# Two PSUM rings for two jobs: the embedding projections beside the last out-projection norm chain, and three norm chains traced between GEMM steps

## The chip, the cores and the metric

One NeuronCore of one Trainium2 chip. The metric is the device time of one execution in microseconds. The kernel before takes 2876.89 us (median of 3 runs, 2875.72 to 2878.07).

## What is computed

One layer of a hybrid encoder, in float32, on two batches with shared weights: a prompt of 512 tokens (P) and a sample of 1024 tokens (S, two groups g of 512). Cut to what matters here:

```python
mix = concat([y_ssd, y_hy], -1) @ w_out                       # 2048 -> 1024, "out-projection"
h = h + rmsnorm(mix, norm_mix_post)
u = rmsnorm(h, norm_ffn_pre)
ff = (silu(u @ w_gate) * (u @ w_up)) @ w_down                 # 1024 -> 2816 -> 1024
h = h + rmsnorm(ff, norm_ffn_post)
gate = sigmoid(rmsnorm(h, ple_norm_pre) @ w_ple_gate)
e = p_l @ w_ple_proj                                          # 256 -> 1024, "embedding projection"
h = h + rmsnorm(gate * e, ple_norm_post)
```

## The kernel before

Matmuls keep float32 accuracy by splitting each operand into a high and a low part and adding three products (`mm3`, L301 to L303). A weight arrives by DMA from the SP queue as `wst`; ScalarE (ACT) copies it into `whi` (L292) and GpSimd (POOL) subtracts to get `wlo` (L293). A streamed activation arrives as `mx` and is split into `mh` (ACT, L325) and `ml` (VectorE, DVE, L326).

The program is written with a tile framework. A tile belongs to a pool and a tag, and a tag owns a fixed number of buffers, a **ring**: a new tile of the tag waits until the tile that held its buffer has been read for the last time. The framework's scheduler orders each engine's instructions once, when the program is built, from the order of the trace, the dependences, and a priority (`high_priority()`); on the chip each engine then runs its list in that order. PSUM's eight banks are three rings: `g` (2 buffers of 2 banks, `gps()`), `a` of pool m (1 bank) and `a` of pool x (3 banks). `aps()` takes `a` from whichever pool `self.apool` names.

After the mixers, the sample's part runs so:

- `out_group(S, 0)` and `out_group(S, 1)`: the out-projection as a streamed GEMM (`stream_gemm`), two column halves of eight steps each. The second half's four accumulators are three `a` of pool x and one `g`.
- After each group `out_post` calls `post`, a **norm chain**: per tile of 128 tokens (order 0, 2, 1, 3) a sum of squares on ACT (L316, into `junk`), the power -0.5 on POOL (L309), scale by the gain row (L1054), add of the residual tile `t` (L1055), which goes to DRAM (L1056), a second sum of squares, scale (L333), and eight transposes on TensorE (L339, from `acc` into two `a`), from which ACT and DVE make the operands `bh` and `bl` of the next GEMM with `stage` and `wsum` between (L129, L137, L325, L326; class `Sums`). `post` is traced as a whole at high priority.
- `ple_proj(S, 0)` and `(S, 1)`: the embedding projection. Per group two loads of p (L1328, into `mx`), two sets of four transposes (L1332, each into one `a`), their split into `mh` and `ml` (128x256), 48 matmuls of 128x512 into four `g`, and eight copies to `mx` (L1346) that go to DRAM as `e` (L1347, issued from the ACT queue). The tag `mx` is a ring of two, and loads and results share it.
- `gate_up`: gate and up as products of a Strassen-like scheme over summed operands (DVE, L1210), a first job on group 0 alone, then one on group 1 alone, then both groups. Its first product's weight sum (`mx<-wst,wst`, L1210) is again a tile of the ring `mx`.
- `down_group(S, 0)`, `(S, 1)`: the streamed GEMM with w_down, then `post` again, then the embedding gate.

In `build`, `self.apool` is pool x from the second half of `out_group(S, 0)` to the end, so the transposes of the norm chains, those of `ple_proj` and the products of `gate_up` all take `a` from the ring of three, in the order of the trace.

Of the kernel before, what the change touches and what calls it, by code (L numbers as in the profile page):

```python
# [18 lines left out]
D = 1024  # L19
# [147 lines left out]
class Kern:  # L167
# [868 lines left out]
    def post(self, pool, acc, row, res, t0, dst, gain=None, u=None, tags=("t4",) * 4, last=False):  # L1036
# [4 lines left out]
        rts = {}  # L1041
# [85 lines left out]
    def ffn(self, q, g, pool, u):  # L1127
# [21 lines left out]
        self.post(pool, acc2, "norm_ffn_post", q.h1, g * 512, q.h2, "ple_norm_pre", v)  # L1149
        return v  # L1150

    def stream_gemm(self, rows, nk, wsrc, evac):


        for nch in range(2):
# [15 lines left out]
            for t in ORDER:  # L1171
                evac(nch, t, pss[t])
            yield
# [19 lines left out]

    def out_group(self, q, g, pool, acc):
# [3 lines left out]
    def out_post(self, q, g, pool, acc):  # L1198
        u = Sums(self, pool)
        self.post(pool, acc, "norm_mix_post", q.x, g * 512, q.h1, "norm_ffn_pre", u)  # L1200
        return u

    def gate_up(self, q, jobs):
# [98 lines left out]
        for job in jobs:  # L1302
            for p in pair(*job):
# [8 lines left out]
    def down_group(self, q, g, pool, u):  # L1312

        acc = self.new_acc(pool)
        for _ in self.stream_gemm(self.streamed(pool, q.hid, g), NF, self.I["w_down"][0], self.keep(acc)):
            pass
        v = u()
        self.post(pool, acc, "norm_ffn_post", q.h1, g * 512, q.h2, "ple_norm_pre", v)
        return v
# [53 lines left out]
    def build(self):  # L1373
# [43 lines left out]
        with self.pool("mix_s", side="right") as mp, ExitStack() as right:  # L1417
# [3 lines left out]
            with self.pool("tail_u") as tu, self.pool("tail_p") as tp:  # L1421
# [12 lines left out]
                u = self.ffn(P, 0, pl, u)  # L1434
# [3 lines left out]
                next(out)  # L1438
                self.ple_post(P, 0, pl, self.ple(P, 0, pl, u))
            self.apool = self.pools["x"][0]  # L1440
            next(out)
            with self.pool("blocks") as tb:
                pb = pm | tags(tb, ("bh", 14), ("bl", 14))
                po |= pb
                us = [self.out_post(S, 0, po, acc)]
                acc = self.new_acc(po)
                for _ in self.out_group(S, 1, po, acc):
                    pass
                us.append(self.out_post(S, 1, po, acc))
                pe = pm | {"et": pm["mx"], "hh": pm["mh"], "hl": pm["ml"]}  # L1450
                for g in range(2):
                    for _ in self.ple_proj(pe, S, g):
                        pass
                right.close()
                with self.pool("hid_s", side="right") as tr:
                    ph = pb | tags(tr, ("wsum", 3), ("sc", 5), ("gt", 6))
                    pe = pb | {"wsum": pm["mx"], "gt": pm["mh"], "sc": pm["ml"]}
                    both = dict(enumerate(us))
                    self.gate_up(S, [(p, m, {g: both[g] for g in gs}) for p, gs, ms in (
                        (pe, [0], (0,)), (ph, [1], (0,)), (ph, [0, 1], range(2, NF, 2))) for m in ms])  # L1460
# [39 lines left out]
```

## Time and profile before

| | |
|---|---|
| median of 3 runs | 2876.89 us |
| the profiled execution | 2871.61 us, its span 2869.8 us |
| TensorE busy | 2685.3 us, 94% of the span |
| VectorE / ScalarE / GpSimd busy | 61% / 46% / 48% |
| mean granted TensorE clock | 0.978 |
| chain that ended last | PE 70%, DVE 14%, DMA 7%, issue 4%, POOL 3%, ACT 2% |

Times inside the profile are microseconds from the span's start. The page has one line per engine with its busy time, the span in 40 slices with the clock that TensorE was granted (9 is 90% or more of the full 2.4 GHz, 5 is half), and the chain of work that ended last. The last out-projection GEMM ends at about 1958, its norm chain and the two embedding projections take the stretch to about 2030, `gate_up` runs to about 2498 and the down-projection from about 2481.

### The profile page before, as it was taken

To read this page: it belongs to the slowest core of one execution; us is meant where nothing else is said; L and a number is where in the kernel's file an instruction comes from. 1 tells how busy PE (TensorE), PEld (TensorE's weight loads), DVE (VectorE), ACT (ScalarE), POOL (GpSimd) and SP (SyncE) were. 2 spreads that over 40 slices of the span, in tenths; PEclk is the share of its full clock that TensorE was granted. 3 is DMA by queue.
4 is the path that set the end of the run, shared out by engine and by line. 5 is a ranking of instruction groups with operands and counts; after the bars stand their busy time and mean duration, and the time that the engine had idled before them with its cause. 6 is when DMAs were issued, how large, how long until landed. Compare 5 with 4: busy or idle time off the path is not lost.

```text
span 2869.8 us, 41652 instructions
## 1 busy us (share of the span) xinstructions
PE 2685.3 (94%) x14696; PEld 2260.9 (79%) x14696; DVE 1753.3 (61%) x2893; ACT 1328.9 (46%) x2564; POOL 1388.9 (48%) x1137
## 2 busy tenths in 40 slices
PE   7999999999999989799999899886799999899998
PEld 5987888778887767588788777664799999877776
DVE  6767996977667887956766742664443434225345
ACT  4534445763333564645444444554433333345453
POOL 4445554433453555534444444553554444445464
PEclk9999999999999999899999999998999999999999
DMA  5545555744335575778888775564332222366664
GB/s 168 179 139 134 150 182 187 219 143 117 110 106 165 169 256 191 221 204 207 195 210 202 184 226 178 191 225 140 102 90 84 79 78 86 122 200 205 204 205 180
DMA packets 446203, 475.85 MB, mean 166 GB/s; under 512 B 29153, under 2 KB 330025, under 8 KB 443691
## 3 DMA queue, kind: packets, MB, share of 16 engines
q1 hardware_dynamic: 340923, 347.34, 39.7%
q0 software_dynamic: 25920, 63.97, 9.9%
q10 hardware_dynamic: 79152, 61.88, 6.8%
q8 instruction: 116, 1.90, 0.3%
q14 instruction: 92, 0.75, 0.1%
HBM read 346.54 MB, written 91.95 MB: 153 GB/s over the span
## 4 chain that ended last, share of the span: by engine, by line
PE 70%; DVE 14%; DMA 7%; issue 4%; POOL 3%; ACT 2%; SPq 0%; DVEq 0%; ACTq 0%; POOLq 0%
PE g L301 18%; PE g L303 17%; PE g L302 17%; PE a L302 3%; PE a L303 3%; PE a L301 3%; DMA mx<-mix_s 2%; PE a L700 2%; PE a L973 1%; DVE E L615 1%; DVE b L692 1%; POOL wlo L293 1%; PE a L628 1%; PE a L404 1%; DVE W L619 1%
## 5 line engine op out<-in xcount | busy, mean ns | idle before, releaser
L293 POOL TENSOR_TENSOR wlo<-wst,whi 128x512 fp32r<-128x512 f32 (+1 forms) x556 | 801.1, 1448 | 778.2 <-ACT whi L292 698.6
L292 ACT ACTIVATE whi<-wst 128x512 fp32r<-128x512 f32 (+1 forms) x556 | 346.7, 629 | 546.5 <-PE g L302 345.6
L301 PE MATMUL g<-uh,whi 128*128 128x512 f32 (+1 forms) x1232 | 493.8, 401 | 8.1 <-DVE cv L393 3.8
L303 PE MATMUL g<-uh,wlo 128*128 128x512 f32 (+1 forms) x1232 | 492.0, 399 | 0.0
L302 PE MATMUL g<-ul,whi 128*128 128x512 f32 (+1 forms) x1232 | 491.3, 399 | 0.0
L301 PE MATMUL g<-bh,whi 128*128 128x256 f32 x1056 | 293.7, 284 | 18.6 <-DVE gt L1210 7.7
L303 PE MATMUL g<-bh,wlo 128*128 128x256 f32 x1056 | 294.5, 281 | 0.8 <-POOL wlo L293 0.8
L302 PE MATMUL g<-bl,whi 128*128 128x256 f32 x1056 | 295.3, 281 | 0.0
L301 PEld LDWEIGHTS g<-uh,whi 128*128 128x128 f32 x1232 | 233.5, 190 | 67.5 <-issue 10.1
L303 PEld LDWEIGHTS g<-uh,wlo 128*128 128x128 f32 x1232 | 232.9, 189 | 54.0 <-issue 5.8
L302 PEld LDWEIGHTS g<-ul,whi 128*128 128x128 f32 x1232 | 233.0, 189 | 53.3 <-issue 6.9
L326 DVE TENSOR_TENSOR ml<-mx,mh 128x512 fp32r<-128x512 f32 x152 | 126.0, 831 | 222.3 <-ACT mh L325 217.9
L393 DVE SCALAR_TENSOR_TENSOR cv<-g,cols,cv 128x510 f32<-128x510 f32 (+3 forms) x192 | 193.0, 1006 | 64.0 <-ACT cv L387 61.9
L285 POOL DMA_DIRECT2D wlo<-wst x132 | 115.7, 934 | 210.0 <-ACT wlo L284 203.3
L301 PEld LDWEIGHTS g<-bh,whi 128*128 128x128 f32 x1056 | 198.2, 190 | 23.7 <-DVE gt L1210 9.9
L303 PEld LDWEIGHTS g<-bh,wlo 128*128 128x128 f32 x1056 | 200.7, 190 | 1.1 <-POOL wlo L293 1.1
L302 PEld LDWEIGHTS g<-bl,whi 128*128 128x128 f32 x1056 | 200.7, 190 | 0.1
L303 PE MATMUL g<-whi,ul 128*128 128x264 f32 (+1 forms) x576 | 190.3, 331 | 1.3 <-DVE rs_t L308 1.3
L302 PE MATMUL g<-wlo,uh 128*128 128x264 f32 (+1 forms) x576 | 191.3, 332 | 0.0
L309 POOL TENSOR_TENSOR rs_t<-rs_t,nhalf 128x1 f32<-128x1 f32 (+2 forms) x112 | 121.1, 1083 | 143.0 <-DVE rs_t L308 141.7
L301 PE MATMUL g<-whi,uh 128*128 128x264 f32 (+1 forms) x576 | 189.3, 330 | 0.0
L301 PE MATMUL g<-whi,mh 128*128 128x512 f32 x412 | 168.7, 409 | 20.0 <-ACT mh L325 14.7
(328 smaller groups left out, 6021.9 us busy)
## 6 DMA issues: line engine op xcount, KB each, us to landing
wst<-in_w_in SPq DMA_DIRECT2D x192, 256.0 KB
wlo<-wst POOLq DMA_DIRECT2D x132, 256.0 KB, 5.0
wst<-in_w_down SPq DMA_DIRECT2D x132, 256.0 KB
wst<-in_w_out SPq DMA_DIRECT2D x96, 256.0 KB
wst<-in_w_gate SPq DMA_DIRECT2D x92, 256.0 KB
wst<-in_w_up SPq DMA_DIRECT2D x92, 256.0 KB
mx<-hid_s SPq DMA_DIRECT2D x88, 256.0 KB
rw<-rows_s SPq DMA_DIRECT2D x32, 512.0 KB
```

What stands on the lines that cost most here:

```text
L285: nc.gpsimd.dma_start(lo, w, accum_op=ALU.add)
L292: nc.scalar.activation(hi, w, AF.Copy)
L293: (eng or nc.gpsimd).tensor_tensor(out=lo, in0=w, in1=hi.bitcast(F32), op=ALU.subtract)
L301: nc.tensor.matmul(ps, lh, rh, start=first, stop=False, skip_group_check=shared)
L302: nc.tensor.matmul(ps, lh, rl, start=False, stop=False, skip_group_check=shared)
L303: nc.tensor.matmul(ps, ll, rh, start=False, stop=last, skip_group_check=shared)
L309: nc.gpsimd.tensor_tensor(out=t[:, :w], in0=t[:, :w], in1=self.nhalf[:, :w], op=ALU.pow)
L326: self.nc.vector.tensor_tensor(out=lo, in0=ps, in1=hi.bitcast(F32), op=ALU.subtract)
L393: nc.vector.scalar_tensor_tensor(out[:, a:b], ps[:, a + d:b + d], wcol(w), out[:, a:b], ALU.mult, ALU.add)
L404: nc.tensor.transpose(ps[:, j * 128:(j + 1) * 128], srcs[i + j], self.ident)
L615: nc.vector.scalar_tensor_tensor(E[:, h], rw[:, 0, h], dbf[:, c, gh:gh + 1], rw[:, 1, h], ALU.add, ALU.min)
L700: nc.tensor.matmul(ps[:, r, c], fw[:, r0 + r, c], sig[:, r0 + r], start=True, stop=True)
```

## The change

Four edits:

1. `post` becomes a generator, `post_steps`, which yields after the first sums of squares and after each tile. For three chains (the prompt's after its FFN, the sample's group 0 after `out_group(S, 0)`, and the sample's group 0 after `down_group(S, 0)`) the steps are now traced between the steps of the GEMM that follows, by `half`, without the high priority. `stream_gemm` yields after every step for that.
2. The last out-projection chain, and that of `down_group(S, 1)`, are traced as a whole at high priority as before (`rush`).
3. `ple_proj(S, 0)`, `ple_proj(S, 1)` and `gate_up`'s first job take `a` from pool m, the ring of one; later jobs take it from pool x as before.
4. The out-projection's own pool is closed before the embedding projections are traced, not after.

No instruction is added or removed: the five engines' lists hold the same rows in another order.

```diff
     @urgent
-    def post(self, pool, acc, row, res, t0, dst, gain=None, u=None, tags=("t4",) * 4, last=False):
+    def post(self, *args, **kw):
+        for _ in self.post_steps(*args, **kw):
+            pass
+
+    def post_steps(self, pool, acc, row, res, t0, dst, gain=None, u=None, tags=("t4",) * 4, last=False):
...
-        rs = {t: self.rstd(self.sumsq(pool, acc[t]), D) for t in ORDER}
+        for t in ORDER:
+            rs[t] = self.rstd(self.sumsq(pool, acc[t]), D)
+        yield
         for i, t in enumerate(ORDER):
             add(t)
             if i > 0:
                 norm(ORDER[i - 1])
                 if i < 3:
                     load(ORDER[i + 1])
+            yield
         norm(ORDER[3])
+        yield
...
+    def half(self, gemm, chain=iter(())):
+
+        for done in gemm:
+            next(chain, None)
+            if done:
+                return
+        for _ in chain:
+            pass
...
         for job in jobs:
+            self.apool = self.pools["m" if job[0] is early else "x"][0]
             for p in pair(*job):
...
+    def rush(self, chain):
+        with self.tc.high_priority():
+            for _ in chain:
+                pass
...
-                us = [self.out_post(S, 0, po, acc)]
+                u0, chain = self.out_post(S, 0, po, acc)
                 acc = self.new_acc(po)
-                for _ in self.out_group(S, 1, po, acc):
-                    pass
-                us.append(self.out_post(S, 1, po, acc))
-                pe = pm | {"et": pm["mx"], "hh": pm["mh"], "hl": pm["ml"]}
-                for g in range(2):
-                    for _ in self.ple_proj(pe, S, g):
-                        pass
+                out = self.out_group(S, 1, po, acc)
+                self.half(out, chain)
+                self.half(out, chain)
+                u1, chain = self.out_post(S, 1, po, acc)
+                self.rush(chain)
                 right.close()
                 with self.pool("hid_s", side="right") as tr:
                     ph = pb | tags(tr, ("wsum", 3), ("sc", 5), ("gt", 6))
                     pe = pb | {"wsum": pm["mx"], "gt": pm["mh"], "sc": pm["ml"]}
-                    both = dict(enumerate(us))
+                    pe |= {"et": pm["mx"], "hh": pm["mh"], "hl": pm["ml"]}
+                    self.apool = self.pools["m"][0]
+                    for g in range(2):
+                        for _ in self.ple_proj(pe, S, g):
+                            pass
+                    both = {0: u0, 1: u1}
...
-                    vs = [self.down_group(S, g, pe, lambda: Quarters(
-                        *[[self.T(pe, [128, 4, 256], t, F32R) for _ in range(4)] for t in ("bh", "bl")]))
-                        for g in range(2)]
-                    for g in range(2):
-                        self.ple_post(S, g, pe, self.ple(S, g, pe, vs[g]))
+                    v0, chain = self.down_group(S, 0, pe)
+                    v1, chain = self.down_group(S, 1, pe, chain)
+                    self.rush(chain)
+                    for g, v in ((0, v0), (1, v1)):
+                        self.ple_post(S, g, pe, self.ple(S, g, pe, v))
```

What this does to the built order. First TensorE's list right behind the last matmul of the out-projection (`g_3656`). The `a` tiles 3789 to 3810 are the norm chain's transposes, 3816 and 3818 those of the embedding projection's group 0, `g_3825` its first result. Before:

```order
L303 MATMUL g_3656_18190<-whi_3751_18547,ml_3746_18536 128x512
L339 MATMUL a_3789_18644<-ident_1_105,acc_3551_17793 128x128 x4
L339 MATMUL a_3791_18651<-ident_1_105,acc_3551_17793 128x128 x4
L339 MATMUL a_3797_18670<-ident_1_105,acc_3553_17795 128x128 x4
L339 MATMUL a_3799_18681<-ident_1_105,acc_3553_17795 128x128 x4
L339 MATMUL a_3804_18711<-ident_1_105,acc_3552_17794 128x128 x4
L339 MATMUL a_3806_18718<-ident_1_105,acc_3552_17794 128x128 x4
L339 MATMUL a_3808_18726<-ident_1_105,acc_3554_17796 128x128 x4
L339 MATMUL a_3810_18737<-ident_1_105,acc_3554_17796 128x128 x4
L1332 MATMUL a_3816_18761<-ident_1_105,mx_3815_18759 128x128 x4
L1332 MATMUL a_3818_18772<-ident_1_105,mx_3817_18770 128x128 x4
L301 MATMUL g_3825_18793<-whi_3820_18783,mh_3811_18755 128x512
```

and with the change, where L1356 is the old L1332:

```order
L303 MATMUL g_3656_18190<-whi_3751_18547,ml_3746_18536 128x512
L1356 MATMUL a_3816_18765<-ident_1_105,mx_3815_18763 128x128 x4
L301 MATMUL g_3825_18797<-whi_3820_18787,mh_3811_18759 128x512
L302 MATMUL g_3825_18797<-wlo_3821_18788,mh_3811_18759 128x512
L303 MATMUL g_3825_18797<-whi_3820_18787,ml_3813_18761 128x512
L301 MATMUL g_3825_18797<-whi_3823_18793,mh_3812_18760 128x512
L302 MATMUL g_3825_18797<-wlo_3824_18794,mh_3812_18760 128x512
L1356 MATMUL a_3818_18776<-ident_1_105,mx_3817_18774 128x128 x4
...
L339 MATMUL a_3789_18644<-ident_1_105,acc_3507_17631 128x128 x4
L339 MATMUL a_3791_18651<-ident_1_105,acc_3507_17631 128x128 x4
L301 MATMUL g_3837_18847<-whi_3832_18837,mh_3811_18759 128x512
L302 MATMUL g_3837_18847<-wlo_3833_18838,mh_3811_18759 128x512
```

The embedding projection's group 0 now starts ahead of the chain's first transposes, and its 48 matmuls stand between the chain's eight sets; group 1 starts behind the last set, as it did.

On ACT the same place. Before, from the split of the weight `wst_3854` on, the chain has the engine to itself for 21 rows:

```order
L292 ACTIVATE whi_3855_18915<-wst_3854_18913 128x512
L316 ACTIVATE junk_3778_18614,ss_3777_18613<-acc_3552_17794 128x1024
L316 ACTIVATE junk_3781_18620,ss_3780_18619<-acc_3554_17796 128x1024
L316 ACTIVATE junk_3784_18629,ss_3783_18628<-t4_3769_18597 128x1024
L316 ACTIVATE junk_3787_18638,ss_3786_18637<-t4_3770_18599 128x1024
L129 ACTIVATE stage_3790_18649<-a_3789_18644 128x512
L325 ACTIVATE bh_3753_18579<-stage_3790_18649 128x4x128
```

and with the change the splits (`mh`), the copies out (L1370, the old L1346) and their stores (L1371, the old L1347) stand between:

```order
L292 ACTIVATE whi_3855_18919<-wst_3854_18917 128x512
L325 ACTIVATE mh_3811_18759<-a_3816_18765 128x256
L316 ACTIVATE junk_3778_18614,ss_3777_18613<-acc_3508_17632 128x1024
L316 ACTIVATE junk_3781_18620,ss_3780_18619<-acc_3510_17634 128x1024
L325 ACTIVATE mh_3812_18760<-a_3816_18765 128x256
L316 ACTIVATE junk_3784_18629,ss_3783_18628<-t4_3769_18597 128x1024
L316 ACTIVATE junk_3787_18638,ss_3786_18637<-t4_3770_18599 128x1024
L325 ACTIVATE mh_3811_18759<-a_3818_18776 128x256
L1370 ACTIVATE mx_3826_18804<-g_3825_18797 128x512
L1371 DMA e_s_82<-mx_3826_18804 128x512
L325 ACTIVATE mh_3812_18760<-a_3818_18776 128x256
L1370 ACTIVATE mx_3827_18813<-g_3825_18797 128x512
```

DVE's list changes in the same way. The lists of the other two chains that are now traced in steps beside the GEMMs of the prompt's tail and of `out_group(S, 1)` stay as they were but for a few neighbours that change places.

Last, the SP queue at the start of the down-projection: gain rows and residual tiles of the next chain, and the streamed activations. Before:

```order
L321 DMA row_4797_25249<-in_norm_ffn_post 128x1024
L321 DMA row_4798_25251<-in_ple_norm_pre 128x1024
L321 DMA row_5117_26463<-in_norm_ffn_post 128x1024
L1045 DMA t4_4799_25253<-h1_s_80 128x1024
L1045 DMA t4_4800_25255<-h1_s_80 128x1024
L1045 DMA t4_4821_25314<-h1_s_80 128x1024
L1187 DMA mx_4548_24275<-hid_s_83 128x512
L1187 DMA mx_4557_24317<-hid_s_83 128x512
```

and with the change, L1196 and L1050 being the old L1187 and L1045:

```order
L321 DMA row_4815_25303<-in_norm_ffn_post 128x1024
L1196 DMA mx_4548_24275<-hid_s_83 128x512
L321 DMA row_4816_25305<-in_ple_norm_pre 128x1024
L321 DMA row_5117_26463<-in_norm_ffn_post 128x1024
L1196 DMA mx_4557_24317<-hid_s_83 128x512
L277 DMA wst_4599_24473<-in_w_down 128x512
L277 DMA wst_4602_24479<-in_w_down 128x512
L1050 DMA t4_4817_25307<-h1_s_80 128x1024
L277 DMA wst_4611_24521<-in_w_down 128x512
L1050 DMA t4_4818_25309<-h1_s_80 128x1024
L1050 DMA t4_4863_25464<-h1_s_80 128x1024
L1196 DMA mx_4560_24323<-hid_s_83 128x512
```

The first streamed block moves from behind six large loads to behind one, the second from behind six to behind three; the third stays behind all six.

## Rows read from the trace of the kernel before

**Rows 1.** The page: the span, each engine's busy time, and the clock that TensorE was granted in 40 slices.

```profile
span 2869.8 us, 41652 instructions
PE 2685.3 (94%) x14696; PEld 2260.9 (79%) x14696; DVE 1753.3 (61%) x2893; ACT 1328.9 (46%) x2564; POOL 1388.9 (48%) x1137
PEclk9999999999999999899999999998999999999999
```

**Rows 2.** Who TensorE waited for from 1955 to 2045: what waited, for what, us in total, times, longest.

```profile
PE a L339 <- DVE acc L333: 14.6, 2, 13.0
PE a L339 <- DVE rs_t L308: 7.0, 1, 7.0
PE a L1332 <- DMA mx<-in_p_sample: 5.4, 2, 4.3
PE g L301 <- ACT mx L1346: 4.6, 7, 1.2
PE g L301 <- ACT ml L1249: 4.1, 1, 4.1
```

**Rows 3.** Busy time by stretch: stretch, its us, busy us of each engine (with instructions), granted clock, DMA share, GB/s.

```profile
1955.00:1972.00 17.00, 4.04 (x19) 3.14 (x18) 12.19 (x14) 9.65 (x18) 10.95 (x10) 0.68 0.32 108
1972.00:1990.00 18.00, 9.10 (x38) 7.55 (x37) 14.91 (x23) 11.18 (x21) 3.74 (x4) 0.59 0.34 117
1990.00:2010.00 20.00, 13.11 (x49) 8.99 (x48) 5.11 (x11) 8.56 (x16) 3.81 (x3) 0.93 0.44 144
2010.00:2030.00 20.00, 16.71 (x68) 12.39 (x68) 2.06 (x5) 5.87 (x13) 0.00 (x0) 0.86 0.29 105
2090.00:2480.00 390.00, 386.60 (x3272) 383.66 (x3271) 157.64 (x173) 134.77 (x233) 188.86 (x137) 1.00 0.28 83
```

**Rows 4.** The chain that ended last, from 1950 to 2050, in order of time: start, us, what.

```profile
1957.20 0.26 PE g L303
...
1972.22 4.42 DMA t<-in_x_sample
...
1989.50 0.79 PE g L301
...
2003.43 2.54 DMA e_s<-mx
2006.06 0.60 ACT mx L1346
2006.68 2.60 DMA e_s<-mx
2009.34 2.65 DMA mx<-in_p_sample
2012.12 1.09 PE a L1332 x4
2013.21 0.43 PE g L301
...
2030.53 2.00 DMA e_s<-mx
2032.70 0.79 DVE mx L1210
```

**Rows 5.** Instructions in order of time around the start of the chain: start, us, engine, line, operation, shapes, count, idle time before and what ended it.

```profile
1957.74 0.40 PE L303 MATMUL g<-whi,ml 128*128 128x512 f32 x1
1960.36 0.64 ACT L292 ACTIVATE whi<-wst 128x512 fp32r<-128x512 f32 x1
1962.73 2.28 DVE L1054 SCALAR_TENSOR_TENSOR acc<-acc,rs_t,row 128x1024 f32<-128x1024 f32 x1 [0.44 <-POOL rs_t L309]
1965.04 1.23 DVE L1055 TENSOR_TENSOR t<-acc,t 128x1024 f32<-128x1024 f32 x1
1971.10 3.65 PE L339 MATMUL a<-ident,acc 128*128 128x128 f32 x16 [12.96 <-DVE acc L333]
```

**Rows 6.** Groups of instructions from 1955 to 2032, shapes kept apart: count, busy us, mean ns of one, idle time before and what ended it.

```profile
L325 ACT ACTIVATE mh<-a 128x256 fp32r<-128x256 f32 x8 | 3.0, 381 | 7.0 <-PE a L1332 5.3 <-DVE ml L326 1.7
L326 DVE TENSOR_TENSOR ml<-a,mh 128x256 fp32r<-128x256 f32 x8 | 3.3, 420 | 18.2 <-ACT mh L325 18.2
L1346 ACT ACTIVATE mx<-g 128x512 f32<-128x512 f32 x16 | 8.9, 595 | 13.7 <-PE g L303 13.3 <-DMA e_s<-mx 0.4
```

**Rows 7.** The start of `gate_up`, instructions in order of time on ACT and POOL.

```profile
2042.57 0.37 ACT L1249 ACTIVATE ml<-g 128x256 f32<-128x256 f32 x1
...
2035.51 5.88 POOL L293 TENSOR_TENSOR wlo<-wst,whi 128x512 fp32r<-128x512 f32 x4
```

**Rows 8.** The start of the down-projection, instructions in order of time on SP, TensorE and ACT; a stretch of the same place by busy time, as in Rows 3.

```profile
2501.30 0.33 SPq L321 DMA_DIRECT2D row<-in_norm_ffn_post  x1
2504.45 0.93 SPq L1187 DMA_DIRECT2D mx<-hid_s  x2
2505.63 0.40 PE L303 MATMUL g<-whi,ml 128*128 128x512 f32 x1
2513.47 0.80 PE L301 MATMUL g<-whi,mh 128*128 128x512 f32 x1 [7.44 <-ACT mh L325]
2517.82 1.30 ACT L325 ACTIVATE mh<-mx 128x512 fp32r<-128x512 f32 x2 [3.68 <-DMA mx<-hid_s]
...
2508.00:2512.00 4.00, 0.00 (x0) 0.00 (x0) 0.00 (x0) 0.00 (x0) 0.08 (x1) 0.83 1.03 396
```

More of the change, by code (lines that the diff above doesn't have):

```diff
@@ L1148, in ffn @@
         v = self.new_u(pool, 4)
-        self.post(pool, acc2, "norm_ffn_post", q.h1, g * 512, q.h2, "ple_norm_pre", v)
-        return v
+        return v, self.post_steps(pool, acc2, "norm_ffn_post", q.h1, g * 512, q.h2, "ple_norm_pre", v)
     def stream_gemm(self, rows, nk, wsrc, evac):
@@ L1170, in stream_gemm @@
                     self.mm3(pss[t], [r[:, t * 128:(t + 1) * 128] for r in lhs[i]], ws[i], k == 0, k == nk - 1)
-            for t in ORDER:
-                evac(nch, t, pss[t])
-            yield
+                if k0 + 2 == nk:
+                    for t in ORDER:
+                        evac(nch, t, pss[t])
+                yield k0 + 2 == nk
     def keep(self, acc):
@@ L1199, in out_post, with gate_up @@
         u = Sums(self, pool)
-        self.post(pool, acc, "norm_mix_post", q.x, g * 512, q.h1, "norm_ffn_pre", u)
-        return u
-    def gate_up(self, q, jobs):
+        return u, self.post_steps(pool, acc, "norm_mix_post", q.x, g * 512, q.h1, "norm_ffn_pre", u)
+    def gate_up(self, q, jobs, early):
         nc, I = self.nc, self.I
@@ L1310, in gate_up, with down_group @@
             pass
-    def down_group(self, q, g, pool, u):
+    def down_group(self, q, g, pool, chain=iter(())):
         acc = self.new_acc(pool)
-        for _ in self.stream_gemm(self.streamed(pool, q.hid, g), NF, self.I["w_down"][0], self.keep(acc)):
-            pass
-        v = u()
-        self.post(pool, acc, "norm_ffn_post", q.h1, g * 512, q.h2, "ple_norm_pre", v)
-        return v
+        gemm = self.stream_gemm(self.streamed(pool, q.hid, g), NF, self.I["w_down"][0], self.keep(acc))
+        for _ in range(2):
+            self.half(gemm, chain)
+        v = Quarters(*[[self.T(pool, [128, 4, 256], t, F32R) for _ in range(4)] for t in ("bh", "bl")])
+        return v, self.post_steps(pool, acc, "norm_ffn_post", q.h1, g * 512, q.h2, "ple_norm_pre", v)
+    def rush(self, chain):
+        with self.tc.high_priority():
+            for _ in chain:
+                pass
     def ple_proj(self, pool, q, g):
@@ L1433, in build @@
                 self.dma_lo = True
-                u = self.ffn(P, 0, pl, u)
+                u, chain = self.ffn(P, 0, pl, u)
                 self.dma_lo = False
@@ L1437, in build @@
                 out = self.out_group(S, 0, po, acc)
-                next(out)
+                self.half(out, chain)
                 self.ple_post(P, 0, pl, self.ple(P, 0, pl, u))
             self.apool = self.pools["x"][0]
-            next(out)
+            self.half(out)
             with self.pool("blocks") as tb:
@@ L1444, in build @@
                 po |= pb
[L1445 removed]
+                u0, chain = self.out_post(S, 0, po, acc)
                 acc = self.new_acc(po)
[L1447 to L1453 removed]
+                out = self.out_group(S, 1, po, acc)
+                self.half(out, chain)
+                self.half(out, chain)
+                u1, chain = self.out_post(S, 1, po, acc)
+                self.rush(chain)
                 right.close()
```

4 lines of the change are left out of this document (2 added, 2 removed).

## The prediction

> **What bounds the kernel now.** I read the page first: TensorE is busy for 94% of the span, at nearly full clock [rows 1], so time can come only from stretches in which it is idle or slowed. The stretches show where those are. From 2090 to 2480 it is busy for 386.6 of 390.0 us at clock 1.00; from 1955 to 1990 it is busy for 13 of 35 us at 0.68 and 0.59 [rows 3]. The waits of 1955 to 2045 name what it waited for: 21.6 us for the scale step and the power step of the norm chain, 5.4 us for the loads of p, 4.6 us for copies to `mx`, 4.1 us for a copy in `gate_up` [rows 2]. Last, the chain that ended last: the GEMM's last matmul at 1957.2, then norm-chain steps only until 1989.50, where the embedding projections' first matmul starts, and then their matmuls, copies, stores and loads until 2032.5 [rows 4]. So two pieces of work run one behind the other: a norm chain of 32 us that leaves TensorE idle, and two projections of 43 us that don't need the chain. They are in line because all their transposes take `a` from one ring in the order of the trace.
>
> **The change part by part.** No row is added, so the cost is all in what now waits for what. The change is worth what the order makes of three places.
>
> *The last norm chain.* I walk through the new order with the old durations. Group 0's first transposes follow the last matmul, which ends at 1958.1 [rows 5], and take 1.09 us [rows 4]: 1959.3. ACT gives `mh` (0.38) behind the weight split of 1960.36, so at 1961.4; DVE gives `ml` (0.42) behind the scale step that starts at 1962.73 and takes 2.28, so at 1965.4, and the second `ml` one add (1.23) later, at 1967.3 [rows 5, 6]. Pool m has one bank, so the second set of transposes waits for that: 1968.4. A ring of three would not have waited; here it costs little, since TensorE has nothing else. From then on the 48 matmuls, 0.23 us apart, are 11.2 us of work, and the chain's eight sets about 8 (sixteen transposes took 3.65 [rows 5]). Three `ml` on DVE ahead of the chain's first scale by the second gain put the chain's first transposes from 1971.1 to 1971.9. Its second half waits for two residual tiles, whose loads (4.42 us before DVE goes on [rows 4]) start as much later. On ACT eight copies (0.60 each [rows 6]), four `mh` and eight store issues stand among the chain's steps, some 9 us; carried through, the chain's last two scales come 3 to 4 us later than before and its last transposes end at about 1991. That costs nothing by itself: its operands are group 1's, which `gate_up`'s first job doesn't read. The ring `mx` of two decides the rest. A copy needs its buffer's store to have landed, 2.54 to 2.60 us from its issue [rows 4], and the copies wait in ACT's list behind chain steps; I get the last copy of group 0 at about 1992 instead of 2006.06. Group 1's loads then need a store and a load, 2.6 and 2.65 us [rows 4], one behind the other: its two sets of transposes come at about 1995 and 1999 where they came at 2009.9 and 2012.12. Seven matmuls now stand ahead of the second set, and the first six after 2012.12 ran at half clock, 0.43 apart [rows 4], which costs 1.2 us that a busier TensorE may keep. From there the list is the old one. I take **14 us**. Bounds: nothing, if filler and chain only take turns; 28 us, if the 43 us of projections began at 1961 with nothing of the chain in their way.
>
> All that follows hangs on the projections' end: the first weight sum of `gate_up` waits for `mx` until 2032.7 [rows 4], and the weights' buffers come free by its own steps, so it moves along.
>
> Here a rule speaks against the change. What the rows show: each copy followed its matmuls, and only 0.4 us of ACT's idle time before the sixteen copies was for a store [rows 6]. The Trainium skill, Perfetto Trace Analysis, section Per-engine timelines, says that ScalarE, VectorE and GpSimd take their instructions strictly in order and TensorE nearly so. By that rule a copy that waits for a store now holds the norm chain behind it; in my walk it does so three times in group 0, and the rule taken to its end is the slow rival below. The Trainium skill, DMA: Bandwidth & Descriptors, section Anatomy of one DMA, gives a transfer a fixed cost of about 2.0 us; that would make each of these three waits 0.6 us shorter than the rows do and the gain an estimated 16 us. The rows decide.
>
> *The start of `gate_up`.* TensorE stood 4.1 us for a copy that ended at 2042.94 behind a weight split on ACT [rows 2, 7]. In the new list that copy stands one place earlier, where its input is ready, 3 us sooner. But POOL's splits run back to back there, four in 5.88 us [rows 7], in an unchanged order, and TensorE, at 1.4 us for a product of twelve, would soon wait for them. Between 0 and 3 us I take **1**, near POOL's row. Against it stands pool m's single bank for the two products that take an `a`; the second needs the first read by DVE, which came long before its weight was split, so 0.
>
> *The start of the down-projection.* TensorE stops at 2506.0 and waits 7.44 us for the first `mx`, issued at 2504.45 behind six loads of 512 KB [rows 8]; the engines move 396 GB/s there. Now it stands behind one load: 0.75 MB from 2501.3, so landed by about 2505.5 and split by 2507. The second block, behind three, comes at about 2510.4. The third stays behind everything, 4.6 MB at that rate, and comes at about 2517.5, as before (2517.82 [rows 8]). So TensorE does two blocks earlier and waits 4 us ahead of the third. Before, the third started at about 2520.9: 2513.47, 24 matmuls of 0.23, and 1.8 us for half clock. The gain is 3.4 us, or 1.7 if the new wait brings the half clock too (7.4 us of idling did [rows 8]). I take **2**.
>
> *The three chains traced in steps.* Two of them keep their order but for neighbours that change places, and the GEMMs beside them cover those: 0, with 1 us either way. The third is the one whose loads moved above. Closing the pool earlier frees space that only `gate_up`'s second job takes, 20 us later: 0.
>
> Sum: 17 us. The profiled execution took 2871.6 by its own time (span 2869.8), so 2854.6; the median of the runs is 5.3 above that execution. **Predicted: 2860 us.**
>
> **The rivals.** *Less overlap* (0.13). TensorE, thinly loaded from 1959 to 1975, stays at half clock through group 0, as it was at 0.68 and 0.59 [rows 3]. The 48 matmuls then take 0.43 instead of 0.23, 9.6 us more, of which about half lies in waits; with nothing gained at the down-projection the gain is 8: 2869. For it: the clock of those rows. Against it: the waits for DVE and the loads are there anyway.
>
> *More overlap* (0.08). The copies on ACT slip in without waits and group 0 keeps its own pace: 25 us, 2852. Against it: the second residual loads, which nothing hastens.
>
> *Slower: the chain and the filler hold each other* (0.05). Place: ACT between 1961 and 1995. If each of group 0's copies waits its 2.6 us for a store with the chain's step behind it, and TensorE's next filler matmul waits for a `g` that this copy frees, the 32 us and group 0's 17 run in line as before, and the single bank adds its wait twice: 8 us from 1959.3 to 1967.3, 3 to 4 in group 1. The forecast turns at the point where group 0's last copy comes after 2006; with both waits unhidden that gives some 8 us more, 2885. Against it: only three of eight copies meet a store in the walk.
>
> *Nothing moves* (0.04): TensorE's list has changed, but if the filler is late (p not loaded, weights not split) the chain comes first all the same, and what the down-projection gains at its start is lost to DMA at the third block: 2876. Against it: p's loads were issued before 1955.
>
> **How the numbers follow.** About 0.2%, 5.8 us, is what a measurement of this kernel can tell from no change. The forecast (a gain of 10 to 23 us) has 0.70. More overlap is all faster; of less overlap (2 to 10 us) about two thirds are. Faster: 0.70 + 0.08 + 0.09 = 0.87. Same: 0.04 + 0.04 = 0.08. Slower: 0.05. The range takes in most of less overlap and of more, 2851 to 2871.
>
> **What would show it.** Right: TensorE's wait of 13.0 us for the scale step falls to the few us around the chain's first transposes; embedding matmuls stand between the chain's transposes; the second loads of p are issued at about 1992 to 1996 and the first sum of `gate_up` comes near 2018; idle time at the down-projection's start breaks in two. Wrong: the chain's last transposes after 2000, ACT idle for stores with chain steps behind them, or a new wait at `gate_up`'s start that takes back what came before.

## The result and the profile after

The changed kernel takes 2862.46 us (median of 5 runs, 2855.3 to 2865.8), the kernel before 2876.89 (5 runs beside it). The ratio is 0.9944, with a 95% interval of 0.9928 to 0.9960: 11.5 to 20.7 us faster. The forecast was 2860, with a range of 2851 to 2871.

The profiled execution took 2855.3 us, 16.3 less than that of before. It is the lowest of the five, so places are compared inside it and not against the median. The page, as in [rows 1]:

```profile
span 2853.5 us, 41647 instructions
PE 2691.4 (94%) x14696; PEld 2264.9 (79%) x14696; DVE 1751.1 (61%) x2893; ACT 1328.7 (47%) x2564; POOL 1389.5 (49%) x1137
PEclk9999999999999999989999999998899999999999
```

The shares hardly move; the gain has to be looked for by place. Four marks cut both traces: A, the out-projection's last copy (ACT `acc<-g`); B, `gate_up`'s first weight sum (DVE `mx<-wst,wst`); C, its last product (DVE `gt<-g,gt`); D, the 91st split of a streamed activation (DVE `ml<-mx,mh`). In order of time, the first three of before:

```profile
1959.88 0.60 ACT L1177 ACTIVATE acc<-g 128x512 f32<-128x512 f32 x1
...
2029.64 0.69 DVE L1210 TENSOR_TENSOR mx<-wst,wst 128x512 f32<-128x512 f32 x1 [14.68 <-DMA e_s<-mx]
...
2491.38 0.69 DVE L1210 TENSOR_TENSOR gt<-g,gt 128x512 f32<-128x512 f32 x1 [2.90 <-PE g L303]
```

and all four of the change:

```profile
1958.61 0.60 ACT L1186 ACTIVATE acc<-g 128x512 f32<-128x512 f32 x1
...
2013.27 0.69 DVE L1227 TENSOR_TENSOR mx<-wst,wst 128x512 f32<-128x512 f32 x1 [12.90 <-DMA e_s<-mx]
...
2476.53 0.69 DVE L1227 TENSOR_TENSOR gt<-g,gt 128x512 f32<-128x512 f32 x1 [2.94 <-PE g L303]
...
2552.22 0.69 DVE L326 TENSOR_TENSOR ml<-mx,mh 128x512 fp32r<-128x512 f32 x1 [0.50 <-ACT mh L325]
```

D of before is at 2568.91. The differences of the marks:

| stretch | before | change | moved | forecast |
|---|---|---|---|---|
| start to A | 1959.9 | 1958.6 | -1.3 | 0 |
| A to B, last chain and projections | 69.8 | 54.7 | -15.1 | -14 |
| B to C, `gate_up` | 461.7 | 463.3 | +1.5 | -1 |
| C to D, start of the down-projection | 77.5 | 75.7 | -1.8 | -2 |
| D to the end | 300.9 | 301.3 | +0.4 | 0 |

The stretches that answer to [rows 3], each placed 1.4 us earlier (columns as there):

```profile
1953.60:1970.60 17.00, 11.34 (x38) 7.69 (x37) 12.34 (x17) 11.56 (x23) 10.23 (x10) 0.70 0.37 123
1970.60:1988.60 18.00, 12.10 (x56) 9.14 (x55) 12.44 (x18) 12.04 (x23) 5.68 (x6) 0.91 0.60 206
1988.60:2008.60 20.00, 15.68 (x59) 10.73 (x58) 9.75 (x17) 9.80 (x19) 1.26 (x1) 0.83 0.36 126
...
2073.00:2463.00 390.00, 386.90 (x3269) 383.97 (x3267) 159.81 (x175) 135.97 (x235) 188.78 (x137) 1.00 0.27 82
```

In the first two TensorE is now busy for 23 of 35 us instead of 13, and in the second its clock is 0.91 instead of 0.59. TensorE's waits from 1955 to 2030 answer to [rows 2] (what waited, for what, us in total, times, longest):

```profile
PE g L301 <- ACT mx L1370: 5.9, 5, 3.2
PE g L301 <- DVE mh L1227: 3.8, 1, 3.8
PE g L301 <- ACT mh L325: 3.2, 2, 2.8
PE g L303 <- DVE rs_t L308: 2.9, 1, 2.9
PE a L1356 <- DMA mx<-in_p_sample: 2.8, 1, 2.8
...
PE a L339 <- DVE acc L333: 1.4, 1, 1.4
```

The 21.6 us for the chain's scale and power steps are 1.4 plus a wait of 2.9 that has the power step's name but ends with an `ml` behind a scale on DVE. The wait for a copy is longer than it was. TensorE's list, in order of time, against the times of [rows 4, 5]:

```profile
1956.69 0.60 PE L1356 MATMUL a<-ident,mx 128*128 128x128 f32 x4
...
1965.76 1.09 PE L1356 MATMUL a<-ident,mx 128*128 128x128 f32 x4
...
1971.22 1.03 PE L339 MATMUL a<-ident,acc 128*128 128x128 f32 x8
...
1989.48 1.04 PE L339 MATMUL a<-ident,acc 128*128 128x128 f32 x8
...
1993.27 0.66 PE L1356 MATMUL a<-ident,mx 128*128 128x128 f32 x4 [2.75 <-DMA mx<-in_p_sample]
...
1997.48 1.09 PE L1356 MATMUL a<-ident,mx 128*128 128x128 f32 x4 [0.36 <-DVE ml L326]
```

The chain's last transposes before, for comparison:

```profile
1985.38 2.32 PE L339 MATMUL a<-ident,acc 128*128 128x128 f32 x8 [1.65 <-DVE acc L333]
```

The chain's transposes begin where they did, at 1971, and its last ones end at 1990.5 instead of 1987.7; between them group 0 of the projections is done. Group 1's two sets come at 1993 and 1997 instead of 2010 and 2012.

### The profile page after: what moved, and what is told of

It is laid out like the page before. It is cut to its first block, busy times and chain, and to the rows that moved or that the text cites. A ratio compares the mean times of both kernels' runs of the same rounds, so it can differ in the third digit from the quotient of the medians.

```text
span 2853.5 us, 41647 instructions
## 1 busy us (share of the span) xinstructions
PE 2691.4 (94%) x14696; PEld 2264.9 (79%) x14696; DVE 1751.1 (61%) x2893; ACT 1328.7 (47%) x2564; POOL 1389.5 (49%) x1137
## 4 chain that ended last, share of the span: by engine, by line
PE 71%; DVE 14%; DMA 6%; issue 4%; POOL 2%; ACT 2%; SPq 1%; DVEq 0%; POOLq 0%; ACTq 0%
PE g L301 18%; PE g L303 17%; PE g L302 17%; PE a L301 3%; PE a L302 3%; PE a L303 3%; PE a L700 2%; DVE E L615 1%; PE a L973 1%; DVE b L692 1%; PE a L628 1%; PE a L404 1%; DVE W L619 1%; DVE ml L326 1%; POOL wlo L293 1%
```

## The experiments

All stand beside runs of the kernel before on the same chip. They ran on three chips, so from one experiment to another the ratios count more than the medians; places come from one profiled execution of each kernel. The first four take the change apart.

**The ring alone.** The kernel before with one edit:

```diff
+                self.apool = self.pools["m"][0]
                 for g in range(2):
                     for _ in self.ple_proj(pe, S, g):
                         pass
+                self.apool = self.pools["x"][0]
```

> The kernel before with one edit: the two embedding projections take `a` from pool m; `gate_up` takes all its products from pool x, and no chain is traced in steps. Theory (the ring alone joins the chain and the projections): from the last copy of the out-projection to `gate_up`'s first weight sum 55 us, as with the whole change (54.7), not 69.8 as before; from the last `gt` product of `gate_up` to the 91st `ml` of the streamed activations 77.5 us as before, since the down-projection keeps its old load order; time 2863 to 2866. Rival (the steps and the earlier closed pool are needed too): the first stretch stays above 62 us and the time within 3 us of the kernel before.

Measured: 2864.09 us, ratio 0.9951 (0.9935 to 0.9967); A to B 54.1, C to D 77.4. The ring alone makes the overlap, and all of it.

**The steps alone.** The change without its ring of one:

```diff
-                    self.apool = self.pools["m"][0]
                     for g in range(2):
...
-            self.apool = self.pools["m" if job[0] is early else "x"][0]
+            self.apool = self.pools["x"][0]
```

> The whole change, but the embedding projections and `gate_up`'s first job take `a` from pool x as before. Theory: the first stretch is 69 to 70 us again, the stretch around the start of the down-projection 75.7 instead of 77.5, and the time 1 to 3 us below the kernel before, which the runs can hardly tell from no change. Rival (the steps themselves let the projections in): the first stretch falls below 65 us.

Measured: 2875.15, ratio 0.9993 (0.9980 to 1.0006); A to B 70.2, C to D 75.8. Its waits from 1955 to 2030 are those of [rows 2]:

```profile
PE a L339 <- DVE acc L333: 14.6, 2, 13.0
PE a L339 <- DVE rs_t L308: 6.8, 1, 6.8
PE a L1356 <- DMA mx<-in_p_sample: 5.8, 2, 4.6
```

So the steps move the start of the down-projection, by 1.7 us, and nothing else that shows, and the two parts add up. The chain's priority has no part in it: built without `rush` for this chain, or with the projection of group 0 traced ahead of the chain, all five engines' lists are row for row those of the change (built, not run).

**`gate_up`'s first job on the ring of three:**

```diff
-            self.apool = self.pools["m" if job[0] is early else "x"][0]
+            self.apool = self.pools["x"][0]
```

> The whole change, but `gate_up`'s first job takes `a` from pool x; the lists of all engines stay word for word those of the change. Theory 1 (the 1.5 us that `gate_up` took longer come from copies and the table load on ACT and from TensorE's clock, not from the ring of one): from the first weight sum to `gate_up`'s last product 463 us as with the change, time within 2 us of the change. Theory 2 (the single bank makes a product wait): that stretch falls to 461 or 462 us and the idle time of 3.8 us ahead of a product in the first job goes.

Measured: 2867.84, ratio 0.9962 (0.9945 to 0.9979); B to C 465.6, with a wait of 4.4 us in the first job. The single bank is not what `gate_up` lost; theory 2 is out. Theory 1's figure was 2.6 us too low and the median is 5 us above the change's, so it is not confirmed by this run. Since the lists are the change's, row for row, this pair also shows how far two executions of one order lie apart by place: 7.2 us before A, 0.2 from A to B, 2.3 in `gate_up`.

**The rings exchanged:**

```diff
                 u1, chain = self.out_post(S, 1, po, acc)
+                self.apool = self.pools["m"][0]
                 self.rush(chain)
...
-                    self.apool = self.pools["m"][0]
+                    self.apool = self.pools["x"][0]
...
-            self.apool = self.pools["m" if job[0] is early else "x"][0]
+            self.apool = self.pools["x"][0]
```

> The whole change with the rings exchanged: the last out-projection chain takes `a` from pool m (one bank), the embedding projections and all of `gate_up` from pool x (three). Theory (any two rings do, the chain isn't what bounds the projections): first stretch 53 to 56 us, with the wait of 2.85 us for the second set's bank gone and the chain's last transposes some us later; time within 3 us of the change. Rival (a chain on one bank is slow, and its steps on ACT and DVE hold the copies): 58 us or more, time over 2866.

Measured: 2863.53, ratio 0.9950 (0.9933 to 0.9966); A to B 55.5. Any two rings do. The wait for the second set's bank didn't go as expected: TensorE waits 2.86 us at the same place for the same `ml` on DVE, bank or not.

The next three ask what still holds the projections beside the chain. The rows are from ACT's list of the change, around the longest of TensorE's waits (3.18 us, to 1979.85):

```profile
1974.36 0.60 ACT L1370 ACTIVATE mx<-g 128x512 f32<-128x512 f32 x1 [0.90 <-PE g L303]
1975.73 1.06 ACT L316 ACTIVATE junk<-t 128x1024 bf16<-128x1024 f32 x1 [0.77 <-DVE t L1060]
1975.80 0.33 ACTq L1371 DMA_DIRECT2D e_s<-mx  x1
...
1979.20 0.60 ACT L1370 ACTIVATE mx<-g 128x512 f32<-128x512 f32 x1 [0.28 <-DMA e_s<-mx]
```

Between the two copies stand a sum of squares that waits 0.77 us for a residual sum, and four splits. When ACT had done them, at 1978.92, the second copy waited 0.28 us more: the store that it needs, issued at 1971.36, landed at 1979.12.

**The stores on SP:**

```diff
-                    nc.scalar.dma_start(q.e[...], et)
+                    (nc.sync if q is self.S else nc.scalar).dma_start(q.e[...], et)
```

> The whole change, but the stores of the sample's embedding projections (`e_s`) are issued from the SP queue instead of ACT's. Theory (a store issued from ACT waits behind a norm-chain step in ACT's list, which waits for a residual tile; so the next copy and TensorE wait): TensorE's wait of 3.2 us for a copy around the middle of group 0 falls to about 1.5 us, and the stretch from the out-projection's last copy to `gate_up`'s first weight sum goes from 54.7 to 52 or 53 us. Rival (SP's list holds loads that wait for weight buffers, and the stores now wait behind those): 56 us or more.

Measured: 2858.33, ratio 0.9933 (0.9918 to 0.9947); A to B 51.1. The stretch fell by more than expected, but the wait named for it stayed: 3.45 us. Here the copy stands behind the chain's steps alone: its store landed at 1982.34 and it began at 1986.18. Where the 3.5 us went is only partly seen: they are shared between the groups (1.7 and 1.8 us, table below), and TensorE is at half clock for 10 instead of 20 us.

**p in buffers of its own:**

```diff
-            st = self.T(pool, [128, 2, 256], "et")
+            st = self.T(pool, [128, 2, 256], ("hh" if t == 0 else "hl") if q is self.S else "et")
```

> The whole change, but the loads of p take the third buffers of the rings `mh` and `ml` instead of sharing the ring `mx` of two with the results. Theory (the ring `mx` of two sets the pace of the second group: its loads wait for a store): the wait of 2.7 us for p goes, the stretch is 52 to 53 us. Rival (the first loads now wait for the out-projection's own `mh` and `ml`, and start 3 us late, and the second set of transposes for the one bank): 55 to 57 us.

Measured: 2856.33, ratio 0.9931 (0.9915 to 0.9947); A to B 49.2, less than expected; group 1 16.1 instead of 22.3 us. Group 1 was paced by the ring `mx` of two, whose buffers p's loads shared with the results; three of the four other kernels with p in its own buffers have 16.1 to 16.3 there (table below).

**Both:**

> Both of the last two edits. If both waits are real and lie one behind the other on TensorE's way: 49 to 51 us, and a time of 2858 to 2860. If they hide one another, or the chain's own pace on DVE and ACT is what holds both: 52 to 54 us.

Measured: 2851.58 (2849.41 to 2855.69), ratio 0.9915 (0.9902 to 0.9929), the lowest median of all, though its interval overlaps those of the two edits alone. The time was better than forecast and the reason wasn't the one given: A to B is 50.7, inside the 49 to 51 expected but no less than with p alone, so moving the stores adds nothing there. The rest came from `gate_up`, 459.2 us instead of 465.1: it is written in yet another order here.

That puts the question on `gate_up`. Its first job stands in one of two orders on TensorE in all kernels of the table below but this one. In the old one TensorE waits for a copy early (4.07 us, the copy of [rows 7]). In the new one the copy comes sooner, and a product of twelve matmuls is moved ahead; then TensorE waits for the DVE sum of the next copy, and that copy stands behind a table load and a silu. In the change, on ACT and TensorE:

```profile
2026.84 1.28 ACT L1305 ACT_TABLE_LOAD   x1
2028.13 0.42 ACT L1305 ACTIVATE mh<-mh 128x256 f32<-128x256 f32 x1
2028.46 0.36 ACT L1266 ACTIVATE ml<-g 128x256 f32<-128x256 f32 x1
...
2029.33 0.58 PE L301 MATMUL g<-bh,whi 128*128 128x256 f32 x1 [3.81 <-DVE mh L1227]
```

**An early silu,** so that the table is loaded during the out-projection:

```diff
                 self.half(out, chain)
+                w = self.T(self.sp, [128, 1], "ss")
+                self.nc.scalar.activation(w, self.nhalf[:, :1], AF.Silu)
                 self.half(out, chain)
```

> The whole change with one more instruction: a silu of one column on ACT during the last out-projection, whose result nothing reads, so that ACT loads its silu table (1.28 us) there and not in `gate_up`. It also makes the scheduler write `gate_up`'s first job in its old order on TensorE and ACT. Theory (what `gate_up` lost with the change, 1.5 to 3.8 us, came from the new order of its first job): from the first weight sum to `gate_up`'s last product 461 to 462 us, as in both kernels with the old order (461.74), 1 us less if the table load was on the way. Rival (it comes from weights that are not there yet, now that `gate_up` starts 15 us sooner, or from TensorE's clock after a different past): 463 to 465 us in the old order too.

Measured: 2856.38, ratio 0.9931 (0.9916 to 0.9947); B to C 460.2. In the old order `gate_up` takes 1.5 us less than before, about the table load, though it starts early.

**The early silu where the new order stays,** on the kernel with both edits:

> The stores on SP, p in its own buffers and the early silu, on top of the change. The scheduler writes `gate_up`'s first job on TensorE in the order of the change (the new one) here. Theory (that order costs 2 to 4 us): stretch of the projections 50 us as with the two edits, from the first weight sum to `gate_up`'s last product 462 to 464 us, and so slower than the two edits alone in spite of the table load taken out: 2853 to 2856. Rival (the table load is what matters): 458 to 460 us, and a time of 2849 to 2851.

Measured: 2858.98, ratio 0.9922 (0.9904 to 0.9940); B to C 461.6, so 2.4 us more than without the silu, just under the theory's range and above the rival's. If the table load is worth what it was above, the order more than undid it; the projections' stretch, at 52.8, missed its 50, and so the time its 2853 to 2856.

**The early silu and p's buffers, in the old order:**

> p in its own buffers and the early silu, on top of the change, with the stores on ACT. `gate_up`'s first job has its old order on TensorE. Theory of the order: stretch of the projections 49 us, `gate_up` 460 us, so 5 to 6 us less than p in its own buffers alone: 2849 to 2852. Rival: `gate_up` as with p in its own buffers alone, 464 to 465 us, time 2854 to 2857.

Measured: 2857.64, ratio 0.9922 (0.9903 to 0.9940). B to C is 460.6 as forecast; A to B is 52.7 and not 49, all of it in group 0, and so the time missed.

**The early silu on the kernel before,** which has the new order though `gate_up` starts as late as before:

> The kernel before with the early silu alone: chain and projections in line as before, `gate_up` begins 15 us later than with the change, but its first job stands in the new order on TensorE and ACT. Theory of the order: from the first weight sum to `gate_up`'s last product 463 to 464 us against 461.74 before, though the table load is gone; time 2877 to 2879, hardly told from no change. Rival (the earlier start, not the order, costs `gate_up` its time): 460.5 to 461.7 us, time 2875 to 2876.

Measured: 2877.48, ratio 0.9991 (0.9979 to 1.0004); B to C 463.0, 1.3 us more than before without a table load in it. The earlier start can't be what costs here, and the order fits. But 1.3 us is less than the 2.3 us between two executions of one order, so the case rests on the groups below and not on this run.

**The residual tile freed at once,** on p in its own buffers:

```diff
-                nc.vector.tensor_tensor(out=rt, in0=a, in1=rt, op=ALU.add)
+                nc.vector.tensor_tensor(out=a if free else rt, in0=a, in1=rt, op=ALU.add)
+            if free:
+                rt = rts[t] = a
```

> p in its own buffers (stores on ACT), and the last out-projection chain writes the residual sum into `acc` instead of the residual tile, which is then free at once: the third and fourth residual loads no longer wait for the chain's first two norms. `gate_up`'s first job stands in the old order on TensorE and ACT, its table load included. Theory (what still holds the projections beside the chain is ACT's list, in which copies stand behind a sum of squares that waits for a residual load): the loads are issued 3 to 5 us earlier, ACT's idle time for the residual sums (2 to 4 us) goes, and the stretch from the out-projection's last copy to the first weight sum is 45 to 48 us (49.2 without the edit); `gate_up` 461.7 us; time 2848 to 2851. Rival (the chain now waits for the store of `acc` ahead of the norm that overwrites it, and holds the copies in its place): 49 to 52 us, time 2852 to 2855.

Measured: 2854.32, ratio 0.9921 (0.9902 to 0.9939); A to B 51.5. SP issues the two loads (`t`) early:

```profile
1963.10 0.34 SPq L1050 DMA_DIRECT2D t<-in_x_sample  x1
...
1967.34 0.34 SPq L1050 DMA_DIRECT2D t<-in_x_sample  x1
```

against, without the edit,

```profile
1971.43 2.05 SPq L1050 DMA_DIRECT2D t<-in_x_sample  x2
```

and group 0 is 1.7 us shorter, but group 1 is 4.1 us longer, with a new wait of 2.0 us for an `ml` and 6.8 us at half clock that begin in it. Stretch and time are those of the rival, but not by its mechanism: no wait of the chain for a store of `acc` shows. The wait was real and its removal bought nothing in sum.

All stretches (us; A to the eighth copy is group 0, from there to B group 1):

| kernel | group 0 | group 1 | `gate_up` | order, table load in it | C to D |
|---|---|---|---|---|---|
| before | 46.2 | 23.6 | 461.7 | old, yes | 77.5 |
| steps alone | 45.9 | 24.3 | 461.7 | old, yes | 75.8 |
| before, early silu | 44.9 | 24.8 | 463.0 | new, no | 77.7 |
| ring alone | 31.2 | 22.9 | 464.7 | new, yes | 77.4 |
| the change | 32.4 | 22.3 | 463.3 | new, yes | 75.7 |
| job on three banks | 31.5 | 23.3 | 465.6 | new, yes | 75.7 |
| rings exchanged | 30.0 | 25.5 | 465.2 | new, yes | 77.4 |
| stores on SP | 30.7 | 20.5 | 464.9 | new, yes | 75.5 |
| p's buffers | 33.0 | 16.1 | 465.1 | new, yes | 77.1 |
| p's buffers, `t` freed | 31.3 | 20.2 | 462.2 | old, yes | 77.1 |
| both edits | 34.3 | 16.3 | 459.2 | a third, yes | 77.6 |
| both, early silu | 36.6 | 16.2 | 461.6 | new, no | 75.2 |
| early silu | 30.8 | 21.5 | 460.2 | old, no | 74.8 |
| p's buffers, early silu | 36.6 | 16.1 | 460.6 | old, no | 76.8 |

With the table load the old order takes 461.7 to 462.2 us and the new one 463.3 to 465.6; without it 460.2 to 460.6 and 461.6 to 463.0. The groups don't overlap, though they are small: three kernels against six, and two against two. The clock is not what parts them: TensorE spent 10.2 us of `gate_up` at half clock both before (461.7) and with the stores on SP (464.9).

## Why the prediction held, and where it did not

The sum was 17 us and the profiled pair shows 16.3; the medians differ by 14.4.

**The last norm chain: right, 15.1 for 14.** The walk also met its times. Taken 1.3 us earlier, as mark A came, it gave 1970.6 for the chain's first transposes (1971.2 in the trace), 1990.7 for the last copy of group 0 (1991.0), 1993.7 and 1997.7 for group 1's sets (1993.3 and 1997.5). The ring-alone kernel shows that this term needs no other edit.

Inside it one step was wrong. I had copies of group 0 wait three times for a store of `mx`, some 2.6 us each; ACT was idle 0.3 us for stores in the whole stretch (sixteen copies):

```profile
L1370 ACT ACTIVATE mx<-g 128x512 f32<-128x512 f32 x16 | 9.2, 594 | 11.0 <-PE g L303 10.5 <-DMA e_s<-mx 0.3
```

Two things stood in its place. The copies stand in ACT's list behind the chain's own steps, and transfers took longer than in the rows of before. The fourth residual load took 7.68 us where it had taken 4.42, as the chain of waits tells:

```profile
1971.62 7.68 DMA t<-in_x_sample
```

The store issued at 1971.36 took 7.8 us until it released the fourth copy (1979.20, shown above), where the walk had 2.6. The trace tells of each landing in 16 updates: of this store the twelfth came at 1974.98 and the last at 1979.12, so most of it had landed long before. ACT was free for that copy at 1978.92, so here list and store held it about equally, and the idle time of 0.28 us doesn't tell how late the store was. In the ring-alone kernel it was the list: the store landed at 1980.91, the copy began at 1983.62, behind the chain's splits.

The DMA share of that stretch had gone from 0.34 to 0.60. Fewer waits of ACT for stores and slower transfers have opposite signs, so the total owes them some luck. The rule of strict order (the Trainium skill, Perfetto Trace Analysis, section Per-engine timelines) agrees with the trace, only the other way round: it was not the chain that stood behind a waiting copy, but copies behind a waiting chain. In the kernel with both edits this is plainest; TensorE waits 4.30 us for a copy that stands behind a sum of squares, and this for a residual sum:

```profile
1986.63 1.06 ACT L316 ACTIVATE junk<-t 128x1024 bf16<-128x1024 f32 x1 [1.83 <-DVE t L1060]
...
1987.69 0.58 ACT L1370 ACTIVATE mx<-g 128x512 f32<-128x512 f32 x1
...
1988.32 0.65 PE L301 MATMUL g<-whi,mh 128*128 128x512 f32 x1 [4.30 <-ACT mx L1370]
```

Taken to its end, as in my slow rival, the rule would have put group 0's last copy after 2006; it came at 1991.

Three smaller readings of the prediction were off. The row at 2032.70 of [rows 4] is `gate_up`'s second weight sum; the first stood at 2029.64, so the sign "near 2018" was one for the second, which came at 2016.38, and the first came at 2013.27. The second set of transposes did not wait for the one bank until 1968.4: five matmuls stand ahead of it in the list, and it came at 1965.76 without a wait. And the 16 us worked out from the fixed cost of a transfer were worked out wrongly. The Trainium skill, DMA: Bandwidth & Descriptors, section Anatomy of one DMA, gives that cost for transfers issued by GpSimd and adds the bytes at 436 GB/s; so a store of 256 KB comes to an estimated 2.6 us, no less than the rows had. Between A and B of this trace the stores issued by ACT took from 2.0 us to the 7.8 above.

**The start of `gate_up`: wrong, in sign too.** I forecast 1 us less and it is 1.5 more (3 to 4 in the five other kernels with the same order on TensorE and the table load in it). The step that failed: I priced the one copy that moved up against POOL's splits, and did not follow what the same order puts next on ACT, the table load and the silu ahead of the following copy. The wait of 4.07 us became one of 3.81, later in the list. Granted clock and matmuls in the first 35 us from B on, before,

```profile
2029.64:2064.64 35.00, 27.78 (x203) 26.94 (x203) 21.57 (x22) 17.61 (x34) 29.17 (x21) 0.90 0.32 95
```

and with the change,

```profile
2013.27:2048.27 35.00, 26.43 (x168) 25.27 (x168) 18.29 (x20) 16.23 (x31) 27.02 (x19) 0.81 0.30 88
```

show 35 matmuls fewer at a lower clock. At 0.12 us each that is an estimated 4 us, of which 1.5 are left at C. POOL's splits, whose row I had taken for the limit, made TensorE wait once, for 0.8 us, as before.

**The start of the down-projection: right at mark D, 1.8 for 2.** The one wait of 7.44 us of [rows 8] is now three, one ahead of each block:

```profile
2492.35 0.50 PE L301 MATMUL g<-whi,mh 128*128 128x512 f32 x1 [1.18 <-ACT mh L325]
2495.66 0.50 PE L301 MATMUL g<-whi,mh 128*128 128x512 f32 x1 [0.23 <-ACT mh L325]
2502.23 0.55 PE L301 MATMUL g<-whi,mh 128*128 128x512 f32 x1 [3.51 <-ACT mh L325]
```

Counted from the issue of the first load (2501.30 before, 2486.43 now), the walk's 2507, 2510.4 and 2517.5 came out as 2507.2, 2510.5 and 2517.1. I had priced the case in which the half clock comes with the new wait at 1.7. It did: 3.4 us of half clock here, 6.8 before.

The gain is not steady, though. Five of the eleven kernels with the new order of loads have 76.8 to 77.6 from C to D, among them the one with the rings exchanged, with 6.8 us of half clock again. Taken from C to the end of the kernel it shows in the mean: 377.9 to 378.5 us in the three kernels with the old order of loads, 374.3 to 378.1 in the eleven with the new one, 376.8 in the mean, 1.5 less.

**The steps of the other chains: right, nothing.** Between the marks the steps-alone kernel differs from before by more than 0.5 us only at the down-projection.

Of the rivals, "nothing moves", the slow one and less overlap are out; less overlap wanted half clock through group 0, and it was 13.7 of 32.4 us. More overlap was to be had: with p in buffers of its own A to B is 20.6 us shorter than before; my bound had been 28.

## What to carry to other kernels

Where two pieces of work don't need each other and still run in line, look for the ring that both take from; a ring of its own, of one bank or of three, was worth 14 to 16 us here, and beside it neither the chain's priority nor the order of the trace changed a row of the built lists. When a stretch gets shorter, follow the new list beyond the place that moved: `gate_up` gave back 1.5 to 4 us because the scheduler wrote its first job anew. Rings that loads and results share are the next thing to part: with p in buffers of its own, stores on another queue and a luckier order of `gate_up`, the kernel takes 2851.58 us, 25 less than before. Against the change that is a ratio of 0.9915 beside 0.9944, and the two intervals just touch.

## What the runs showed that was not expected

The order of one job is worth as much as most edits tried here (1 to 4 us), and unrelated edits change it: one silu of one column, two stages earlier, turned it round in the change and in the kernel before, in opposite directions. A comparison of two versions of such a kernel should set the engines' lists side by side first, and times by place second.

Group 0 takes 30 to 32 us in some kernels with the overlap and 36.6 in two others, and the place of this is in TensorE's list. The transposes of the chain's third tile stand behind 42 of the group's 48 matmuls in the change and in every kernel where p shares the ring `mx`, behind 30 with p's buffers alone (33.0) and with both edits (34.3), behind 24 in the two with 36.6. There TensorE stands still at these transposes for 4.15 us and, with both edits and the early silu, for 6.42:

```profile
1987.16 1.23 DVE L1060 TENSOR_TENSOR t<-acc,t 128x1024 f32<-128x1024 f32 x1 [3.21 <-DMA t<-in_x_sample]
...
1990.39 1.28 DVE L333 SCALAR_TENSOR_TENSOR acc<-t,rs_t,row 128x1024 f32<-128x1024 f32 x1 [0.57 <-POOL rs_t L309]
...
1991.82 1.94 PE L339 MATMUL a<-ident,acc 128*128 128x128 f32 x8 [6.42 <-ACT mx L1370]
```

The profile names a copy on ACT that ended just before, but these transposes read `acc`, whose scale on DVE ended at 1991.67, and ahead of it in its list DVE had waited 3.21 us for a residual load. With the residual tile freed the transposes stand behind 23 matmuls, the loads come early, TensorE doesn't wait there, and group 0 takes 31.3 us. So filler covers a chain's wait only as far as TensorE's list puts it ahead of the step that waits. No run moved these transposes alone, so this is read from lists and waits and not shown by an edit. Why the fourth residual load takes 4.4 us in one kernel and 7.7 in another stays open.
